# The second feed-forward layer's two products as seven block products each, in two phases with the inner operands in DRAM

## The chip, the cores and the metric

One core of a Trainium2 chip runs the whole program in one launch. The time is device microseconds per execution; the value given is the median of the runs. A profiled execution is a run of its own, and every row below comes from it.

## The reference

Two layers over 1024 latent tokens of width 1024 with 256 context tokens ahead. Each layer is a mixer followed by a squared-ReLU feed-forward part of inner width 4096. The change touches the feed-forward part of the second layer, which sees the 1024 latent tokens alone:

```python
def modulate(x, shift, scale):
    return rms_norm(x) * (1.0 + scale) + shift

def squared_relu_mlp(h, w1, w2):
    return jnp.square(jax.nn.relu(h @ w1)) @ w2
...
# x = x + gate * squared_relu_mlp(modulate(x, shift, scale), w1, w2)
```

All arithmetic is float32. With h as 1024x1024 and w1 as 1024x4096, each of the two products is as large as 4 x 1024^3 multiply-adds.

## The kernel before

Activations are held transposed: eight tiles x (channel blocks of 128 partitions), 1024 tokens along the free dimension. TensorE multiplies in a one-pass 32-bit format, so every float32 operand is split into a high part (a copy by ACT, L94) and a low part (raw minus high, by POOL unless another engine is named, L95), and a product takes three matmuls: high by high, high by low, low by high. `mmk` writes these three for every 512-column chunk (L110).

`wo_phase` ends the mixer: `out_proj` adds the output projection to x one channel block at a time, and `Stats` sums the squares on TensorE. `mlp_layer` then runs the feed-forward part. `norm_mod` multiplies x by rstd on DVE (L226), makes the high part on ACT (L227), the modulated value on DVE (L228) and the low part on POOL (L229), in 16 pieces of 512 columns. `mlp` walks over 32 row blocks f of w1. `first(f, k)` accumulates over the eight channel blocks into two PSUM banks, ACT applies ReLU and the square (L261, L262), DVE makes the low part (L266, L267), and `second(f, c)` multiplies with row f of w2: for each of the eight output blocks three matmuls per chunk into a fresh bank, which DVE adds into x at once (L280). Weights come one row block ahead by `load_w`: one 512 KB transfer on SP's queue, a 1024-wide split on ACT and POOL.

The order of the work on each engine is set by a scheduler from the code, the tile pools and its own estimate of durations; each engine runs its list in order. SP issues all transfers, also in order. PSUM has eight banks, given out in turn.

Of the kernel before, what the change touches and what calls it, by code (L numbers as in the profile page):

```python
# [6 lines left out]
F32 = mybir.dt.float32  # L7
F32R = mybir.dt.float32r
# [962 lines left out]
def mlp_layer(kk, xt, n, mods, w1, w2, segs, stats, side=None, done=None):  # L971

    tc = kk.tc
    with tc.tile_pool(name="MH", reuse_waits="tile", bufs=16) as H:
        kk.slab_w = n
        hs = [tuple(kk.slab(n, F32R, "h", pool=H) for _ in range(2)) for _ in range(KC)]
        with tc.tile_pool(name="MR", reuse_waits="tile", bufs=1) as S, tc.tile_pool(name="MN", reuse_waits="tile", bufs=2) as T:
            kk.S, kk.T = S, T
# [1112 lines left out]
```

## Time and profile before

| | |
|---|---|
| median of 3 runs | 4363.31 us (4356.72 to 4365.94) |
| the profiled execution | 4363.96 us |
| its span | 4362.2 us |
| PE busy | 4064.2 us, 93% |
| DVE, ACT, POOL busy | 59%, 38%, 29% |
| the last feed-forward layer | 3638.0 to the end of the span |

Times in the rows count from the start of the span. In a row of a timeline, the bracket at the end gives the idle time ahead of the instruction and what ended it; `x2` means two instructions merged into one row. PE is the matmul, PEld the weight load that runs beside it, and PEclk the clock that TensorE was granted, 1.00 for 2.4 GHz and 0.50 for 1.2 GHz.

### The profile page before, as it was taken

The numbers are of one execution on the slowest core, as the hardware profiler recorded it, in microseconds if no ns is written. First come the engines' busy times: TensorE is split into PE (matmuls) and PEld (weight loads), VectorE is DVE, ScalarE is ACT, GpSimd is POOL, SyncE is SP. The second block draws the span as 40 slices with busy tenths as digits, with TensorE's granted clock in tenths as the row PEclk, the third lists the DMA queues.
The fourth block names the chain that finished last, engine by engine and source line by source line (L and its number), as shares of the span: only waits on it lengthen the run. The fifth ranks groups of instructions, "written<-read, shape, count | busy, mean of one in ns | idle before, by whom it ended". The sixth has DMA issues, their size and how long they took to land. (4 is left out here: it accounts for less than half of the span.)

```text
span 4362.2 us, 70943 instructions
## 1 busy us (share of the span) xinstructions
PE 4064.2 (93%) x27277; PEld 3262.2 (75%) x27277; DVE 2555.5 (59%) x4810; ACT 1652.6 (38%) x4159; POOL 1280.2 (29%) x1526
## 2 busy tenths in 40 slices
PE   6999998998999999997989985999999998999999
PEld 3899875676777888884757754878777865888887
DVE  4320265517556666668684427678777526666666
ACT  4132365513111111115655533666666632111111
POOL 4112010114111111115533335555545323222221
PEclk9999998999999999998979996999999999999999
DMA  4414344511222111112333454445444431111111
GB/s 171 121 60 138 87 151 140 186 39 33 86 85 63 38 36 39 39 39 70 98 118 111 155 188 114 120 128 136 129 129 130 108 114 44 49 49 49 49 49 63
DMA packets 389183, 409.12 MB, mean 94 GB/s; under 512 B 149884, under 2 KB 305820, under 8 KB 388844
## 3 DMA queue, kind: packets, MB, share of 16 engines
q1 hardware_dynamic: 388844, 404.58, 30.8%
q8 instruction: 215, 3.52, 0.3%
q14 instruction: 124, 1.02, 0.1%
HBM read 304.71 MB, written 95.57 MB: 92 GB/s over the span
## 5 line engine op out<-in xcount | busy, mean ns | idle before, releaser
L280 DVE SCALAR_TENSOR_TENSOR x<-m,mods,x 128x512 f32<-128x512 f32 x1280 | 824.1, 690 | 572.1 <-PE m L110 571.9
L95 POOL TENSOR_TENSOR wl<-raw,wh 128x1024 fp32r<-128x1024 f32 (+1 forms) x236 | 507.6, 2154 | 1919.7 <-ACT wh L94 1872.3
L94 ACT ACTIVATE wh<-raw 128x1024 fp32r<-128x1024 f32 (+1 forms) x236 | 221.7, 940 | 1368.1 <-PE m L110 1068.5
L110 PE MATMUL m<-h,wh 128*128 128x512 f32 (+1 forms) x2560 | 632.2, 375 | 26.9 <-POOL h L229 19.4
L110 PEld LDWEIGHTS m<-h,wh 128*128 128x128 f32 x2560 | 450.2, 189 | 149.5 <-POOL h L229 29.7
L110 PE MATMUL m<-hidh,wh 128*128 128x512 f32 x1280 | 357.8, 372 | 5.7 <-DVE x L280 5.7
L110 PE MATMUL m<-hidl,wh 128*128 128x512 f32 x1280 | 355.5, 371 | 0.8 <-DVE hidl L267 0.7
L110 PE MATMUL m<-hidh,wl 128*128 128x512 f32 x1280 | 352.9, 370 | 0.0
L110 PE MATMUL m<-h,wl 128*128 128x512 f32 x1280 | 352.8, 372 | 0.0
L377 PE MATMUL pt<-wh,h 128*128 128x256 f32 x1600 | 289.3, 283 | 0.0
L110 PEld LDWEIGHTS m<-hidh,wh 128*128 128x128 f32 x1280 | 224.4, 188 | 56.6 <-DVE x L280 13.7
L110 PEld LDWEIGHTS m<-hidl,wh 128*128 128x128 f32 x1280 | 224.8, 188 | 44.6 <-DVE hidl L267 2.2
L110 PEld LDWEIGHTS m<-h,wl 128*128 128x128 f32 x1280 | 225.1, 189 | 42.3
L110 PEld LDWEIGHTS m<-hidh,wl 128*128 128x128 f32 x1280 | 224.4, 188 | 42.9 <-issue 0.5
L377 PEld LDWEIGHTS pt<-wh,h 128*128 128x128 f32 x1600 | 250.0, 192 | 0.0
L1496 DVE TENSOR_TENSOR prd<-P,R 80x31 f32<-80x31 f32 (+15 forms) x496 | 213.5, 430 | 24.8 <-POOL TT L1511 7.8
L377 PE MATMUL pt<-wl,h 128*128 128x256 f32 x800 | 226.4, 283 | 0.0
L1497 DVE TENSOR_TENSOR R<-R,prd 80x31 f32<-80x31 f32 (+15 forms) x496 | 218.6, 441 | 9.6
L1457 PE MATMUL G<-AR,BK 64*128 64x128 f32 x1280 | 173.3, 334 | 22.0 <-POOL AR L1446 10.4
L1018 POOL TENSOR_TENSOR ss<-h 128x512 f32<-128x512 f32 (+1 forms) x128 | 154.5, 1216 | 121.2 <-DVE xt L1021 96.9
L1464 DVE TENSOR_TENSOR G<-G,c_gmask 128x512 f32<-128x512 f32 (+1 forms) x160 | 98.8, 630 | 142.4 <-PE G L1457 142.3
L1457 PEld LDWEIGHTS G<-AR,BK 64*128 64x128 f32 x1280 | 119.8, 209 | 52.6 <-issue 15.9
(403 smaller groups left out, 8203.7 us busy)
## 6 DMA issues: line engine op xcount, KB each, us to landing
raw<-in_w SPq DMA_DIRECT2D x128, 512.0 KB
araw<-in_ada_w SPq DMA_DIRECT2D x80, 512.0 KB
kar<-rw_kar SPq DMA_DIRECT2D x64, 384.0 KB
css<-rw_css SPq DMA_DIRECT2D x80, 256.0 KB
x<-in_xT SPq DMA_DIRECT2D x16, 640.0 KB
raw<-in_w_v SPq DMA_DIRECT2D x20, 512.0 KB
rw_css<-rs SPq DMA_DIRECT2D x16, 640.0 KB
UV<-rw_v SPq DMA_DIRECT2D x80, 128.0 KB
```

The source lines that it names most:

```text
L94: self.nc.scalar.activation(hi, raw, AF.Copy)
L95: (eng or self.nc.gpsimd).tensor_tensor(lo, raw, hi.bitcast(F32), ALU.subtract)
L110: mm(o[:M, :b - a], ww, xx[:, a:b], start=(first and p == 0), stop=(last and p == 2))
L280: V.scalar_tensor_tensor(xt[c][:, u:v], p[:, u - a:v - a], gate[:, c, cond:cond + 1], xt[c][:, u:v], ALU.mult, ALU.add)
L377: mm(ps[:, :n], xx[:, sl], ww[:, k % 4, :], start=(k == 0 and p == 0), stop=(k == KC - 1 and p == 2))
L1018: nc.gpsimd.tensor_tensor(S, h[:, q - 1:q - 1 + w], h[:, q + 1:q + 1 + w], ALU.add)
L1457: nc.tensor.matmul(pg[h][:, 128 * j:128 * j + 128], BK[HH[h], j, :], AR[HH[h], j, :], start=True, stop=True)
L1464: V.tensor_tensor(G[:, :, h, 0:m], ps.rearrange("q (c t) -> q c t", t=128)[:, :, 0:m], mask[:, :, 0:m], ALU.mult)
L1496: V.tensor_tensor(pr, P3[:, s, s + 1:32].unsqueeze(1).to_broadcast([n_, w, n]), R3[:, 0:w, s].unsqueeze(2).to_broadcast([n_, w, n]), ALU.mult)
L1497: V.tensor_tensor(R3[:, 0:w, s + 1:32], R3[:, 0:w, s + 1:32], pr, ALU.add)
```

## The change

The last layer no longer calls `mlp_layer`. `wino_mlp` computes both products with the Strassen-Winograd scheme: each operand is cut into 2x2 blocks, seven block products of sums and differences replace eight, and the results are combined. `h_blocks` makes seven 512x512 operands B out of h, four tiles of 128 partitions each, split into high and low (28 splits, two lows in five on DVE, the others on POOL). `left_first` loads w1 for row blocks f and f+16 and makes the seven weight operands of f on POOL: four combinations and seven 512-wide splits into a ring of seven buffers. `wino_first` runs over 16 f with the seven products in the order SEQ, 12 matmuls each; products that share a combination accumulate in one PSUM bank, with copies by ACT in between (c1, u2, u3). DVE makes the four squared blocks and four differences, and these seven inner operands per f go to DRAM (`hd`). The stores of the last f are held back to the second phase.

`wino_second` runs four steps s over 16 f: two, two, two and one of the seven products, each accumulated over all f in four PSUM banks. In each iteration the operands are read from `hd` and from w2 in halves of 512 columns, combined on DVE and split, w on POOL, the h tiles on POOL and DVE. x is stored to DRAM by `wo_phase` (`xr`) and reloaded at the start of the second phase; at the end of each step DVE adds the finished blocks into it and they go out in halves.

```diff
+SEQ = (0, 1, 5, 4, 6, 3, 2)
+NRING = 7
+WAHEAD = 4
+def triple(kk, o, w, x, first, last):
+    for p, (ww, xx) in enumerate(((w[0], x[0]), (w[0], x[1]), (w[1], x[0]))):
+        kk.nc.tensor.matmul(o, ww, xx, start=(first and p == 0), stop=(last and p == 2), skip_group_check=True)
+def h_blocks(kk, xt, mods, part, rstd, B):
...
+    def norm(c):
+        x = xt[c][:, :NL]
+        V.tensor_tensor(x, x, rstd, ALU.mult)
+        nc.scalar.activation(x, x, AF.Identity, scale=mods[:, 8 * part + 8 + c, 0:1], bias=mods[:, 8 * part + c, 0:1])
+        return x[:, 0:512], x[:, 512:1024]
...
+    for k in range(4):
+        V.tensor_tensor(half(k, 0), half(k, 0), half(4 + k, 0), ALU.subtract)
+        put(3, k, half(k, 0))
...
+def left_first(kk, w1, groups):
...
+        yield wsplit(kk, r1[:, a])
+        s3 = kk.W.tile([128, 512], F32, tag="s3", name="s3", bufs=2)
+        P.tensor_tensor(s3, r1[:, a], r2[:, a], ALU.subtract)
+        yield wsplit(kk, r1[:, b])
+        P.tensor_tensor(r2[:, a], r2[:, a], r2[:, b], ALU.add)
+        P.tensor_tensor(r1[:, a], r2[:, a], r1[:, a], ALU.subtract)
...
+def wino_first(kk, left, groups, B, hd):
...
+        elif p == 6:
+            d["u3"] = copy(d.pop("a"), "u3")
+            d["r22"] = square(f, "r22", d["e"], d["u3"], ALU.add)
+            store(2, f, d["r22"])
...
+            V.tensor_tensor(t1, r12, d["r11"], ALU.subtract)
+            store(4, f, t1)
...
+                w = ws.pop(0)
+                for k in range(4):
+                    triple(kk, d[nm], tuple(t[:, 128 * k:128 * k + 128] for t in w), B[p][k], new and k == 0, k == 3)
+                after(f, p)
...
+def wino_second(kk, w2, hd, late, pool, xr, gate, done):
...
+    prods = ((0, 1), (5, 4), (6, 3), (2,))
...
+        elif s == 1:
+            a, b = t[:, 0:512], t[:, 512:1024]
+            V.tensor_tensor(a, a, b, ALU.add)
+            V.tensor_tensor(b, a, keep[f], ALU.subtract)
+            ws = [wsplit(kk, b), wsplit(kk, a)]
+            V.tensor_tensor(sum4[f], sum4[f], a, ALU.subtract)
...
+        return ws, [wsplit(kk, x, V if j else P) for j, x in enumerate(B)]
...
+    for i in range(LO2):
+        load(i)
+    for d, t in late:
+        nc.sync.dma_start(d, t)
+    ready = [operands(0)]
+    for c in range(KC):
+        nc.sync.dma_start(xt[c], xr[c])
...
@@ -1815,10 +2123,11 @@
-        with tc.tile_pool(name="X", reuse_waits="tile", bufs=1) as X:
-            xt, st = wo_phase(kk, I, d, xd, X, kk.mods[1])
-            with tc.tile_pool(name="W", reuse_waits="tile", bufs=4) as kk.W:
-                mlp_layer(kk, xt, NL, kk.mods[1], I["w1_1"], I["w2_1"], SEG1, st, None, lambda c: nc.sync.dma_start(out[c], xt[c]))
+        xt, st = wo_phase(kk, I, d, xd, X, kk.mods[1], xr)
+        wino_mlp(kk, X, xt, kk.mods[1], I["w1_1"], I["w2_1"], st, xr,
+                 lambda x, c, h: nc.sync.dma_start(out[c][:, 512 * h:512 * h + 512], x))
@@ -1934,8 +2243,9 @@
-        for x in behind(out_proj(kk, I["w_o"], rows(), xt, NL, mods, 2, SEG1, kk.ww), 1):
+        for c, x in enumerate(behind(out_proj(kk, I["w_o"], rows(), xt, NL, mods, 2, SEG1, kk.ww), 1)):
             st.add(x)
+            nc.sync.dma_start(xr[c], x)
```

Three places of the order. The first is POOL at the start of the layer. In its list of before, wl is the low part of a whole weight tile and h a low part of the modulated x:

```order
L1661 TENSOR_TENSOR y_35816<-y_35816,rds 128x512
L1673 TENSOR_TENSOR ro<-ro,gt 128x512 x2
L95 TENSOR_TENSOR wl<-raw,wh 128x1024 x6
L229 TENSOR_TENSOR h<-nt,h 128x512
L95 TENSOR_TENSOR wl<-raw,wh 128x1024 x2
L229 TENSOR_TENSOR h<-nt,h 128x512 x15
L95 TENSOR_TENSOR wl<-raw,wh 128x1024 x60
```

In the list of after, rl is the low part of a weight operand, s and raw are combinations of weights, and b00l is the low part of the first tile of the first h operand:

```order
L1068 TENSOR_TENSOR s_36805<-raw 128x512
L1070 TENSOR_TENSOR raw<-raw 128x512
L1071 TENSOR_TENSOR raw<-raw 128x512
L95 TENSOR_TENSOR rl<-raw,rh 128x512 x2
L1068 TENSOR_TENSOR s_36811<-raw 128x512
L95 TENSOR_TENSOR rl<-raw,rh 128x512
L1070 TENSOR_TENSOR raw<-raw 128x512
L95 TENSOR_TENSOR rl<-raw,rh 128x512
L1071 TENSOR_TENSOR raw<-raw 128x512
L1077 TENSOR_TENSOR raw<-raw 128x512 x2
L95 TENSOR_TENSOR rl<-raw,rh 128x512
L95 TENSOR_TENSOR b00l<-x_35777,b00h 128x512
```

The weight work of the first two row blocks now stands in one piece ahead of the first low part of h.

The second place is PE and ACT within the first two row blocks. ACT of before, where h is the high part of the modulated x and mr and hidh belong to the square:

```order
L227 ACTIVATE h<-nt,mods_70 128x512
L206 ACTIVATE rstd<-rb 128x256
L94 ACTIVATE wh<-raw 128x1024 x2
L227 ACTIVATE h<-nt,mods_70 128x512 x15
L94 ACTIVATE wh<-raw 128x1024
L261 ACTIVATE mr<-m_36627 128x512
```

ACT of after; b33h is the last high part of the h operands in the list, rh the high part of a weight operand:

```order
L94 ACTIVATE b21h<-x_35782 128x512
L94 ACTIVATE b22h<-x_35783 128x512
L94 ACTIVATE b23h<-x_35784 128x512
L94 ACTIVATE b33h<-x_35780 128x512
L94 ACTIVATE rh<-raw 128x512 x2
L1116 ACTIVATE c_36830<-wa 128x512
L1116 ACTIVATE c_36851<-wa 128x512
L94 ACTIVATE rh<-s_36805 128x512
```

PE of before, at the first matmuls of the layer:

```order
L193 MATMUL st<-sq,ones 32x256 x8
L205 MATMUL rb<-r_36511,row_78 128x256 x4
L110 MATMUL m_36627<-h,wh 128x512 x2
L110 MATMUL m_36627<-h,wl 128x512
L110 MATMUL m_36628<-h,wh 128x512
L110 MATMUL m_36635<-h,wh 128x512
L110 MATMUL m_36636<-h,wh 128x512
```

PE of after, behind the first two products (wa and wb); we is the accumulator of the fourth and the last product in SEQ:

```order
L1010 MATMUL wb<-b12h,rl 128x512
L1010 MATMUL wb<-b13h,rh 128x512
L1010 MATMUL wb<-b13l,rh 128x512
L1010 MATMUL wb<-b13h,rl 128x512
L1010 MATMUL we<-b40h,rh 128x512
L1010 MATMUL we<-b40l,rh 128x512
L1010 MATMUL wa<-b50h,rh 128x512
L1010 MATMUL wa<-b50l,rh 128x512
L1010 MATMUL wa<-b50h,rl 128x512
L1010 MATMUL wa<-b51h,rh 128x512
```

The high parts of weights that stood ahead of h on ACT stand behind b33h from the seventh on, and PE's list takes two matmuls of the fourth product, we, ahead of the third, wa.

The third place is SP where the two phases meet. In the list of before SP has one run of weight loads up to the outputs there:

```order
L1933 DMA x_35776<-xd 128x1024
L1913 DMA ct<-rw_cat 128x1024
L90 DMA raw<-in_w_o 128x1024 x2
L90 DMA raw<-in_w_1 128x1024 x64
L1821 DMA out_x<-x_35769 128x1024
L1821 DMA out_x<-x_35770 128x1024
L1821 DMA out_x<-x_35771 128x1024
```

In the list of after, hd_15 are stores of the last row block, k and q halves of w2, x the reload:

```order
L1223 DMA hd_15_36672<-t_39308 128x512
L1223 DMA hd_15_36624<-t_39309 128x512
L1226 DMA x_39358<-xr_35769 128x1024
L1226 DMA x_39359<-xr_35770 128x1024
L1226 DMA x_39360<-xr_35771 128x1024
L1226 DMA x_39361<-xr_35772 128x1024
L1226 DMA x_39362<-xr_35773 128x1024
L1226 DMA x_39363<-xr_35774 128x1024
L1226 DMA x_39364<-xr_35775 128x1024
L1226 DMA x_39365<-xr_35776 128x1024
L1187 DMA k_39322<-in_w_1 128x512
L1187 DMA q_39323<-in_w_1 128x512
```

The last stores and the eight reloads of x stand ahead of the weights of the third iteration of the second phase, which are the k and q in the last two rows.

## Rows read from the trace of the kernel before

**Rows 1.** The page's first part: busy us (share of span) xinstructions.

```profile
PE 4064.2 (93%) x27277; PEld 3262.2 (75%) x27277; DVE 2555.5 (59%) x4810; ACT 1652.6 (38%) x4159; POOL 1280.2 (29%) x1526
```

**Rows 2.** Windows of the last layer's stages: stretch, length, busy by engine, PEclk, DMA.

```profile
core 0: us, PE busy (x) PEld busy (x) DVE busy (x) ACT busy (x) POOL busy (x), PEclk, DMA share, GB/s
3563.50:3625.50 62.00, 62.00 (x261) 43.46 (x260) 5.78 (x9) 7.67 (x18) 2.41 (x2) 1.00 0.03 9
3625.50:3638.00 12.50, 4.62 (x25) 1.47 (x24) 5.46 (x5) 7.60 (x15) 4.65 (x2) 0.79 0.32 88
3638.00:3653.20 15.20, 9.23 (x18) 5.59 (x19) 14.05 (x12) 6.48 (x9) 12.41 (x7) 0.50 0.31 100
3653.20:3687.10 33.90, 27.13 (x110) 19.56 (x108) 28.34 (x30) 13.78 (x20) 23.49 (x14) 1.00 0.10 27
3687.10:4341.50 654.40, 654.40 (x2886) 541.63 (x2887) 424.82 (x605) 121.17 (x177) 139.70 (x58) 1.00 0.15 46
4341.50:4355.30 13.80, 13.80 (x62) 11.12 (x60) 13.74 (x22) 0.82 (x2) 0.00 (x0) 1.00 0.36 148
4355.30:4362.20 6.90, 0.05 (x1) 0.00 (x0) 3.24 (x5) 0.00 (x0) 0.00 (x0) 0.82 0.77 313
```

**Rows 3.** The chain of waits, two pieces: start us, us, what.

```profile
3687.08 654.45 PE m L110 x2885
...
4356.57 1.98 DVE x L280 x3
```

**Rows 4.** Groups by line, 3600 to 4362: busy us, mean ns, idle before.

```profile
L280 DVE SCALAR_TENSOR_TENSOR x<-m,mods,x 128x512 f32<-128x512 f32 x512 | 356.7, 744 | 229.6 <-PE m L110 229.6
L110 PE MATMUL m<-h,wh 128*128 128x512 f32 x1024 | 279.7, 393 | 14.7 <-POOL h L229 9.8 <-ACT h L227 4.8
...
L110 PE MATMUL m<-h,wl 128*128 128x512 f32 x512 | 159.6, 392 | 0.0
...
L266 DVE TENSOR_TENSOR mr<-mr 128x512 f32<-128x512 f32 x64 | 60.5, 983 | 5.6 <-ACT hidh L262 5.6
...
L261 ACT ACTIVATE mr<-m 128x512 f32<-128x512 f32 x64 | 34.3, 588 | 18.9 <-PE m L110 18.9
```

**Rows 5.** Timeline of POOL, 3630 to 3650: start us, us, operation.

```profile
3631.92 4.65 POOL L95 TENSOR_TENSOR wl<-raw,wh 128x1024 fp32r<-128x1024 f32 x2 [57.06 <-ACT wh L94]
...
3640.22 5.57 POOL L95 TENSOR_TENSOR wl<-raw,wh 128x1024 fp32r<-128x1024 f32 x2
```

**Rows 6.** Timeline of DVE, 3598 to 3700.

```profile
3638.46 7.89 DVE L226 TENSOR_TENSOR nt<-x,rstd 128x512 f32<-128x512 f32 x4
...
3656.15 0.68 DVE L226 TENSOR_TENSOR nt<-x,rstd 128x512 f32<-128x512 f32 x1
```

**Rows 7.** Groups by line and shape, the whole span.

```profile
L94 ACT ACTIVATE wh<-raw 128x512 fp32r<-128x512 f32 x64 | 39.9, 625 | 60.5 <-PE po L1065 34.5 <-PE pv L1266 13.3 <-DMA raw<-in_rkv 7.9
...
L1653 POOL TENSOR_TENSOR y<-y,rds 128x512 f32<-128x512 f32 x16 | 18.8, 1178 | 4.2 <-DVE rds L1652 3.3 <-POOL vt L1649 0.3
...
L534 DVE TENSOR_TENSOR raw<-raw,rope 128x1024 f32<-128x1024 f32 x8 | 9.7, 1218 | 0.0
```

**Rows 8.** Timeline of ACT, 3633 to 3645.

```profile
3633.99 0.94 ACT L206 ACTIVATE rstd<-rb 128x256 f32<-128x256 f32 x3 [1.21 <-PE rb L205]
...
3640.45 1.06 ACT L94 ACTIVATE wh<-raw 128x1024 fp32r<-128x1024 f32 x1 [1.27 <-DMA raw<-in_w]
```

**Rows 9.** Timeline of SP's DMA issues, 3630 to 3640 and 4340 to 4362.

```profile
3634.29 2.63 SPq L90 DMA_DIRECT2D raw<-in_w  x2
...
4349.35 9.55 SPq L1821 DMA_DIRECT2D out_x<-x  x8
```

**Rows 10.** Window with the reload of x by the output projection.

```profile
3520.00:3530.00 10.00, 10.00 (x37) 7.92 (x37) 9.00 (x21) 4.17 (x6) 3.44 (x3) 0.82 1.06 387
```

**Rows 11.** Timeline of PE, end of the output projection.

```profile
3619.79 0.63 PE L110 MATMUL wo<-cth,wh 128*128 128x512 f32 x2
...
3624.92 0.63 PE L110 MATMUL wo<-cth,wl 128*128 128x512 f32 x2
```

More of the change, by code (lines that the diff above doesn't have):

```diff
@@ L982, in mlp_layer, with wsplit, wraw @@
             mlp(kk, xt, n, hs, w1, w2, mods[:, 40:48, :], segs, side, done)
+SEQ = (0, 1, 5, 4, 6, 3, 2)
+NRING = 7
+WAHEAD = 4
+HTAGS = ("c1", "u2", "u3", "r11", "r21", "r22")
+def wsplit(kk, src, eng=None):
+    hi, lo = (kk.W.tile([128, 512], F32R, tag=t, name=t, bufs=NRING) for t in ("rh", "rl"))
+    kk.split(src, hi, lo, eng)
+    return hi, lo
+def wraw(kk, src):
+    t = kk.W.tile([128, 1024], F32, tag="raw", name="raw", bufs=4)
+    kk.nc.sync.dma_start(t, src)
+    return t
+def triple(kk, o, w, x, first, last):
+    for p, (ww, xx) in enumerate(((w[0], x[0]), (w[0], x[1]), (w[1], x[0]))):
+        kk.nc.tensor.matmul(o, ww, xx, start=(first and p == 0), stop=(last and p == 2), skip_group_check=True)
@@ new lines, in h_blocks, with put @@
+def h_blocks(kk, xt, mods, part, rstd, B):
+    nc = kk.nc
+    V, P = nc.vector, nc.gpsimd
+    n = [0]
+    def put(p, k, src):
+        n[0] += 1
+        hi, lo = B[p][k]
+        kk.split(src, hi, lo, V if n[0] % 5 in (0, 2) else P)
+    def norm(c):
[4 more added lines that the diff above has]
+    for k in range(4):
+        put(0, k, norm(k)[0])
+    for k in range(4):
+        put(1, k, norm(4 + k)[0])
+    half = lambda c, i: xt[c][:, 512 * i:512 * i + 512]
+    for k in range(4):
+        t = kk.tmp([128, 512], "n1", bufs=2)
+        V.tensor_tensor(t, half(k, 1), half(k, 0), ALU.subtract)
+        V.tensor_tensor(half(k, 0), half(4 + k, 1), t, ALU.subtract)
+        put(5, k, half(k, 0))
+        put(4, k, t)
+    for k in range(4):
+        P.tensor_tensor(half(k, 1), half(4 + k, 1), half(k, 1), ALU.subtract)
+        put(6, k, half(k, 1))
+    for k in range(4):
+        V.tensor_tensor(half(k, 0), half(k, 0), half(4 + k, 0), ALU.subtract)
+        put(3, k, half(k, 0))
+    for k in range(4):
+        put(2, k, half(4 + k, 1))
@@ new lines, in left_first, with load, one @@
+def left_first(kk, w1, groups):
+    P = kk.nc.gpsimd
+    raws = {}
+    fs = [f for g in groups for f in g]
+    def load(f):
+        if f < 16:
+            raws[f] = [wraw(kk, w1[g].rearrange("q k m -> q (k m)")) for g in (f, f + 16)]
+    load(0)
+    def one(f):
+        if f not in raws:
+            load(f)
+        r1, r2 = raws.pop(f)
+        a, b = slice(0, 512), slice(512, 1024)
+        yield wsplit(kk, r1[:, a])
[4 more added lines that the diff above has]
+        P.tensor_tensor(r1[:, a], r2[:, a], r1[:, a], ALU.subtract)
+        yield wsplit(kk, r1[:, a])
+        yield wsplit(kk, r2[:, a])
+        load(f + 1)
+        yield wsplit(kk, s3)
+        yield wsplit(kk, r2[:, b])
+        P.tensor_tensor(r1[:, b], r1[:, b], r1[:, a], ALU.subtract)
+        yield wsplit(kk, r1[:, b])
+    for g in groups:
+        gens = [one(f) for f in g]
+        for _ in SEQ:
+            for x in gens:
+                yield next(x)
@@ new lines, in wino_mlp @@
+def wino_mlp(kk, X, xt, mods, w1, w2, stats, xr, done):
+    tc = kk.tc
+    kk.W = tc.alloc_tile_pool(name="WW", reuse_waits="tile", bufs=1, side="right")
+    H = tc.alloc_tile_pool(name="WH", reuse_waits="tile", bufs=1, side="right")
+    B = [None] * 7
+    for p in SEQ:
+        B[p] = [tuple(H.tile([128, 512], F32R, name="b%d%d%s" % (p, k, x)) for x in "hl") for k in range(4)]
+    groups = [(0, 1)] + [(f,) for f in range(2, 16)]
+    left = left_first(kk, w1, groups)
+    hd = [[kk.dram.tile([128, 512], F32, name="hd%d_%d" % (p, f), tag="hd%d_%d" % (p, f)) for f in range(16)] for p in range(7)]
+    kk.slab_w = NL
+    with tc.tile_pool(name="WN", reuse_waits="tile", bufs=1) as kk.S:
+        kk.T = kk.S
+        h_blocks(kk, xt, mods, 3, stats.rstd(), B)
+    X.release()
+    with tc.tile_pool(name="WT", reuse_waits="tile", bufs=2) as kk.T:
+        late = wino_first(kk, left, groups, B, hd)
+        H.release()
+        with tc.tile_pool(name="WK", reuse_waits="tile", bufs=1, side="right") as pool:
+            wino_second(kk, w2, hd, late, pool, xr, mods[:, 40:48, :], done)
+    kk.W.release()
@@ L1817, in build_full @@
         d = layer1_mixer(kk, I, xt, X, kk.mods[1], st1)
-        with tc.tile_pool(name="X", reuse_waits="tile", bufs=1) as X:
-            xt, st = wo_phase(kk, I, d, xd, X, kk.mods[1])
-            with tc.tile_pool(name="W", reuse_waits="tile", bufs=4) as kk.W:
-                mlp_layer(kk, xt, NL, kk.mods[1], I["w1_1"], I["w2_1"], SEG1, st, None, lambda c: nc.sync.dma_start(out[c], xt[c]))
+        X = tc.alloc_tile_pool(name="X", reuse_waits="tile", bufs=1)
+        xr = [dr.tile([128, NL], F32, name="xr%d" % c, tag="xr%d" % c) for c in range(KC)]
+        xt, st = wo_phase(kk, I, d, xd, X, kk.mods[1], xr)
+        wino_mlp(kk, X, xt, kk.mods[1], I["w1_1"], I["w2_1"], st, xr,
+                 lambda x, c, h: nc.sync.dma_start(out[c][:, 512 * h:512 * h + 512], x))
 RC = ["mu", "w0", "a0", "k_k", "k_a", "lnx_w", "lnx_b", "rks", "sel", "gmask"]
```

144 lines of the change are left out of this document (143 added, 1 removed).

## The prediction, made before the kernel ran

> **What bounds the kernel now.** I read the page's busy shares first: TensorE is busy 93% of the span and no other engine above 59% [rows 1]. The windows by stage then show where that holds [rows 2]. In the last feed-forward layer there is a ragged start from 3638.0, a stretch of 654.4 us with PE busy all of it at granted clock 1.00, and an end of 6.9 us in which PE does nothing. The chain of waits says the same: one piece, 654.45 us, 2885 matmuls [rows 3], so 226.8 ns each. The layer has 1024 + 4 x 512 = 3072 matmuls [rows 4]. Of these 2885 are in that piece, 62 behind it [rows 2], so 125 came before 3687.1; they needed 28.4 us of work and took 49.1. So 20.7 us are lost at the start, and the rest is matmul count times 226.8 ns. The end is VectorE's: its last additions run after the last matmul, the last of the eight output transfers is issued by 4358.9, 3.3 us before the end [rows 9].
>
> **What the change removes.** Each product is now 7 x 16 x 12 = 1344 matmuls, so 2688 instead of 3072. All have the same 128x512 shape, each with its own weight load. The 384 that go are worth 384 x 0.2268 = 87.1 us, the most that can be won on PE. VectorE also loses the 512 additions of 744 ns out of PSUM [rows 4]. The instruction order on every engine is unchanged up to the last eight steps of the output projection, so everything before 3626 stays.
>
> **Start of the layer, the largest loss.** Three steps.
> (a) POOL now does 14 weight operations (six lows, eight combinations) ahead of the first low part of h, b00l. The nearest price is the first pair of 1024-wide subtractions, 4.65 us for two with VectorE out of the way [rows 5]; a 512-wide POOL operation took 1178 ns [rows 7]. When VectorE ran products with two SBUF operands beside them, two such POOL subtractions took 5.57 us [rows 5], and four 512-wide VectorE products took 7.89 us, where one alone takes 0.68 [rows 6]. So they take turns: a 512-wide VectorE operation adds (5.57 - 4.65)/2 = 0.46 us to POOL, and a pair of 512-wide ones, one on each, costs 1.18 + 0.46 = 1.64 us. A 1024-wide VectorE product (1218 ns [rows 7], 0.53 more than the 0.68) makes the pair 2.15 us.
> ACT's rstd copies began at 3633.99 [rows 8]; four 512-wide splits of 625 ns [rows 7] now stand between them, so the first norm starts at about 3638. By then POOL, from about 3631.5, has done 5 or 6 of its 14. The other eight or nine take turns with eight 1024-wide norms and one split: 8 x 2.15 + 1.64 = 18.8, so b00l starts near 3657. Until then PE can do one matmul.
> (b) After that POOL has 21 and VectorE 22 operations before all seven h operands exist, 1.64 us a pair. PE does the first two products as their parts come, 46 matmuls, and then meets a matmul of the fourth product whose weight ACT splits only behind b33h. b33h needs VectorE's twentieth operation: 3657 + 20 x 1.64 = 3690, plus two ACT splits of 0.6, so about 3691.5.
> (c) From there 168 - 46 = 122 matmuls of the first pair of row blocks remain, 27.7 us. PE has then stood for some 20 us. Before, the granted clock was 0.50 (the 1.2 GHz level) from 3638.0 to 3653.2 [rows 2] after a similar gap, with PE starved most of the time. I allow 2 to 3 us for slow matmuls and get 3722 for the end of the first pair.
> PE thus loses 3722 - 3638 - 168 x 0.2268 = 46 us here against 20.7 before. Bounds: 3700, if weights and h are ready some 20 us earlier because the turns cost less; 3735, if each wait adds a little.
>
> **The rest of phase one.** 14 row blocks of 84 matmuls, 19.05 us each. Per block POOL has 11 operations (7 lows, 4 combinations), VectorE 8 with two SBUF operands and 4 out of PSUM. Taking turns: 8 x 1.64 + 3 x 1.18 = 16.7 us of POOL. ACT's ten take 6.2. Transfers are 1 MB of weights and 1.8 MB of intermediates per block, 150 GB/s, where 387 was reached [rows 10]. All hidden under PE, by 2.4 us in the tightest case. I add 3 us for copies that PE waits for: the accumulator of the sixth product must be copied out of PSUM (0.59) and added (0.74) within one product, 2.72 [rows 4].
> The Trainium skill (SBUF — State Buffer, Who interferes with whom) has a rule that speaks against this change: a VectorE instruction with two SBUF inputs and a GpSimd instruction that reads SBUF exclude each other for the whole instruction. By that rule the trace agrees: the turns above are what it describes, and the change puts eight such operations per block beside eleven of POOL.
>
> **The seam between the phases.** SP is one queue. The third iteration's weights (k, q) now stand behind the last stores of phase one, and behind the reload of x, 8 x 512 KB. Call the last matmul of phase one T. The first weights' transfers are issued when block 15's third square is done, T - 1.2, and land about 3 us later: the second of two 512 KB loads, issued by 3636.92 [rows 9], was ready for ACT at 3640.45 [rows 8], 3.5 us, and these have half the size. ACT and POOL then split three tiles before the second matmul can run: T + 1.8 + 0.6 + 3 x 1.18 = T + 6. Two iterations of 24 matmuls give T + 17. The last store waits for VectorE's r12, four differences and one weight combination, about T + 6.5. 4.45 MB at 387 GB/s [rows 10] take 11.5, k and q land at T + 20.5, their lows and that of the h tile follow: T + 25. That is 25 - 11 = 14 us lost, plus 2 for the slower clock after two gaps: 16 us. Bounds 5 (if the reload starts early) and 30.
>
> **Phase two and the end.** Per iteration 24 matmuls, 5.44 us. POOL has 3 splits, VectorE 2 operations with two SBUF operands in steps one and three (4.46 us by turns), 4 in step two: 3 x 1.64 + 0.6 = 5.5, above 5.44. With seven buffers in the ring this is nearly serial: 4 us over step two. Step four has 2 POOL splits in 2.72 us. Changing banks between steps: 2 us. At the end the additions keep pace with PE, and 256 KB instead of 512 go out last: 4.4 us behind the last matmul instead of 6.9.
>
> **Sum.** 3722 + 2520 x 0.2268 (571.5) + 3 + 16 + 4 + 2 + 4.4 = 4322.9, against a span of 4362.2: 39 us less. The profiled execution took 4363.96, 0.65 above the median of the runs, 4363.31. Median after: 4363.3 - 39 = 4324.
> One price has two rows: in the output projection twelve pairs run from 3619.79 to 3624.92, 233 ns a matmul at clock 1.00 [rows 2, 11], not 226.8. I take 226.8, since the matmuls of this layer had it; the other would add 2520 x 0.0064 = 16 us.
> The Trainium skill (TensorE: Matmul & The Clock Gate, Wait — 56ns, not 53.3ns?) gives 215.7 ns for a warm 512-column matmul; by that the 2520 would take 543.6 us. The trace differs: 226.8, and the measurement decides.
>
> **Rivals.**
> 1. Slower: the turns of VectorE and POOL become the bound. The point is 19.05 us a block, a pair of 1.94 us instead of 1.64. If all 12 VectorE operations hold POOL up for their 0.68, a block takes 11 x 1.18 + 12 x 0.68 = 21.1, 2.1 x 14 = 29 us more; an iteration of phase two 3 x 1.18 + 4 x 0.68 = 6.3, 0.8 x 48 = 39 more. Less the 4 counted: 4324 + 64 = 4388. For it: VectorE's L266 takes 983 ns on average beside POOL [rows 4]. Against it: L280, with one SBUF operand, keeps 744.
> 2. The start or the seam costs less: the first pair done at 3700, seam 14: 4300.
> 3. Matmuls at 233 ns: 4340.
> 4. The queue at the seam costs twice, 32 us: 4340.
> That the change would not do what it says is excluded by the order: PE has 384 instructions fewer.
>
> **How the numbers follow.** A difference below 0.2% (8.7 us) counts as none. Forecast, within 4308 to 4338: 0.48. Rivals: 2 0.13, 3 0.11, 4 0.10, 1 0.18. Of rival 1, 0.11 ends above 4372 and 0.07 in between, since a little over the point costs 30 us. Of 3 and 4 together with other small losses 0.02 end within 0.2%. Faster 0.80, same 0.09, slower 0.11. The range leaves out rival 1 and the best of rival 2: 4296 to 4356.
>
> **What would show it.** In the trace of after: the first long run of PE at about 3692 and its second block pair at 3722; blocks 19.05 us apart; one PE gap of some 6 and one of some 8 us at the seam, released by POOL's lows behind k and q; step two slightly over 87 us. The forecast is wrong if blocks are over 20 us apart with PE waiting for POOL, or if PE runs densely before 3680.

## The result and the profile after

The changed kernel took 4329.08 us (median of 8 runs, 4320.61 to 4349.31), the kernel before beside it 4360.02 (8 runs, 4347.85 to 4366.05). The medians are 31 us apart. The ratio is 0.9934, with a 95% interval of 0.9914 to 0.9955: 0.66% faster, clear of noise but small. The forecast was 4324, within 4296 to 4356, and as a difference 39 us.

The profiled execution had a span of 4322.0 us against 4362.2, 40 us less, but 9 of these lie ahead of the layer. ScalarE's first rstd copy, which opens the layer, began at 3624.92, and before at 3633.99 [rows 8]; ahead of it both kernels issue the same work but for eight stores, and in the executions below that copy lies anywhere from 3623.1 to 3638.6, so the 9 us are within what differs from one execution to the next. So from here on times count from that copy, and are called "behind rstd". From it to the end the layer took 728.2 us before and 697.1 after: 31.1 less, what the medians say. By the same count the forecast was 688.9.

The windows by stage of the changed kernel (columns as in [rows 2]; the last row is a short stretch of phase two):

```profile
core 0: us, PE busy (x) PEld busy (x) DVE busy (x) ACT busy (x) POOL busy (x), PEclk, DMA share, GB/s
3644.60:3662.70 18.10, 15.08 (x48) 10.03 (x48) 17.60 (x12) 13.74 (x19) 15.50 (x10) 0.83 0.01 1
3662.70:3681.90 19.20, 0.15 (x1) 0.00 (x0) 18.05 (x14) 8.64 (x16) 16.68 (x12) 0.64 0.00 0
...
3752.00:3983.90 231.90, 231.90 (x1024) 191.80 (x1022) 158.82 (x151) 67.77 (x115) 182.72 (x125) 1.00 0.47 160
3983.90:4013.00 29.10, 17.32 (x59) 13.08 (x59) 20.66 (x18) 8.35 (x15) 16.97 (x12) 0.82 1.01 370
...
4104.70:4108.20 3.50, 3.50 (x9) 2.73 (x10) 2.44 (x4) 0.00 (x0) 0.00 (x0) 0.52 0.65 195
```

They answer [rows 2]. In the first row PE does 48 matmuls, in the second it stands for 19.2 us. The third is a stretch of 231.9 us in which PE is busy all the time. Around 3983.9 lies the seam, with the transfer engines at 100%. In the last row, behind a gap of 4 us, the granted clock is 0.52.

The page's first part, and the longest piece of the chain, answer [rows 1] and [rows 3]:

```profile
PE 3980.1 (92%) x26893; PEld 3190.9 (74%) x26893; DVE 2516.8 (58%) x4533; ACT 1756.3 (41%) x4379; POOL 1654.3 (38%) x1819
```

```profile
4193.89 89.56 PE w L1010 x388
```

PE has 84.1 us less busy time, near the 87.1 expected (busy time overlaps and holds slow matmuls), and it is still what runs longest, but the chain now has one piece of 89.56 us where before it had 654.45. 388 matmuls in 89.56 us are 230.8 ns each with the slow ones in it; twelve of phase one's blocks took 19.04 us for 84, which is 226.7.

Where the time of the layer goes, from the starts of the matmuls (us; the pure work is 3072 or 2688 matmuls of 0.2268):

| | before | forecast | after |
|---|---|---|---|
| pure work | 696.7 | 609.6 | 609.6 |
| lost up to the end of the first pair (before: ahead of the end) | 24.6 | 49.9 | 50.3 |
| lost in the other 14 blocks | | 3 | 3.8 |
| lost at the seam | | 16 | 16.2 |
| lost in phase two behind it | | 6 | 13.3 |
| behind the last matmul | 6.9 | 4.4 | 3.9 |
| layer | 728.2 | 688.9 | 697.1 |

So of the 87.1 us of matmuls that are gone, 56 are given back. The experiments ask what takes them.

### The profile page after: what moved, and what is told of

Same layout as the page of the kernel before. It is cut to its first block, busy times and chain, and to the rows that moved or that the text cites. A ratio compares the mean times of both kernels' runs of the same rounds, so it can differ in the third digit from the quotient of the medians.

```text
span 4322.0 us, 71491 instructions
## 1 busy us (share of the span) xinstructions
PE 3980.1 (92%) x26893; PEld 3190.9 (74%) x26893; DVE 2516.8 (58%) x4533; ACT 1756.3 (41%) x4379; POOL 1654.3 (38%) x1819
## 5 line engine op out<-in xcount | busy, mean ns | idle before, releaser
L280 DVE SCALAR_TENSOR_TENSOR x<-m,mods,x 128x512 f32<-128x512 f32 (+1 forms) x768 | 467.6, 656 | 341.0 <-PE m L110 340.7
L110 PE MATMUL m<-h,wh 128*128 128x512 f32 (+1 forms) x1536 | 352.5, 362 | 12.2 <-POOL h L229 9.7
L110 PEld LDWEIGHTS m<-h,wh 128*128 128x128 f32 x1536 | 256.3, 189 | 88.8 <-issue 26.8
L95 POOL TENSOR_TENSOR rl<-raw,rh 128x512 fp32r<-128x512 f32 x160 | 241.0, 1515 | 119.4 <-ACT rh L94 119.2
L110 PE MATMUL m<-hidh,wh 128*128 128x512 f32 (+1 forms) x768 | 198.3, 360 | 1.9 <-DVE x L280 1.9
L110 PE MATMUL m<-hidl,wh 128*128 128x512 f32 (+1 forms) x768 | 195.6, 358 | 0.3 <-DVE hidl L267 0.3
L110 PE MATMUL m<-hidh,wl 128*128 128x512 f32 (+1 forms) x768 | 193.8, 357 | 0.0
L110 PE MATMUL m<-h,wl 128*128 128x512 f32 (+1 forms) x768 | 193.0, 359 | 0.0
L1010 PE MATMUL w<-rl,rh 128*128 128x512 f32 x448 | 178.5, 399 | 11.8 <-DVE rl L95 7.7
L1010 PE MATMUL w<-rh 128*128 128x512 f32 x448 | 176.9, 395 | 7.8 <-ACT rh L94 7.8
```

The lines of the kernel that those rows point to most:

```text
L95: (eng or self.nc.gpsimd).tensor_tensor(lo, raw, hi.bitcast(F32), ALU.subtract)
L110: mm(o[:M, :b - a], ww, xx[:, a:b], start=(first and p == 0), stop=(last and p == 2))
L280: V.scalar_tensor_tensor(xt[c][:, u:v], p[:, u - a:v - a], gate[:, c, cond:cond + 1], xt[c][:, u:v], ALU.mult, ALU.add)
L1010: kk.nc.tensor.matmul(o, ww, xx, start=(first and p == 0), stop=(last and p == 2), skip_group_check=True)
```

## The experiments

Only the layer's time is compared where a kernel has a single execution, since the part ahead of it differs by several microseconds from one execution to the next. The layer's own time moves a little too, so such a run is read at the place that its edit touches.

### The reload of x later

```diff
-    for c in range(KC):
-        nc.sync.dma_start(xt[c], xr[c])
...
         load(i + LO2)
+        if 3 <= i < 3 + KC:
+            nc.sync.dma_start(xt[i - 3], xr[i - 3])
```

> The reload of x (eight 512 KB transfers) is issued one per iteration behind the loads of iterations 3 to 10 of phase two, instead of ahead of the third iteration's weights. Theory (SP's order): in the changed kernel the third iteration's weights k and q were issued at 3995.03, behind 4.9 us of reload; now they are issued some 5 us earlier, the two PE gaps of 2.44 and 2.48 us in iteration 2 and the slow clock behind them go, iteration 2 takes 5.4 to 6 us instead of 9.35, and the phase starts 4 us shorter. The first two gaps (6.13 and 2.79 us) stay, since they hang on the first weights' landing and POOL's first lows. Rival (POOL and the port): POOL needs 1.7 us for each of three lows per iteration whenever VectorE works beside it, so iteration 2 still takes over 8 us.

SP's queue in the changed kernel, first the reload, then the third iteration's first weight:

```profile
3990.06 4.92 SPq L1226 DMA_DIRECT2D x<-xr  x8
3995.03 0.43 SPq L1187 DMA_DIRECT2D k<-in_w  x1
```

PE at the seam and behind it in the changed kernel (the bracket is the idle time and what ended it):

```profile
3983.57 0.39 PE L1010 MATMUL we<-b23h,rl 128*128 128x512 f32 x1
3989.70 0.79 PE L1010 MATMUL w<-rh 128*128 128x512 f32 x1 [5.75 <-ACT rh L94]
3992.50 0.79 PE L1010 MATMUL w<-rl,rh 128*128 128x512 f32 x1 [2.00 <-POOL rl L95]
...
4006.99 0.51 PE L1010 MATMUL w<-rh 128*128 128x512 f32 x1 [2.06 <-ACT rh L94]
4009.47 0.79 PE L1010 MATMUL w<-rl,rh 128*128 128x512 f32 x1 [1.98 <-POOL rl L95]
...
4104.70 0.67 PE L1010 MATMUL w<-rl,rh 128*128 128x512 f32 x1 [3.56 <-DVE rl L95]
```

The first two gaps are the ones ended at 3989.70 and 3992.50, the next two at 4006.99 and 4009.47. Gaps in the text, here and below, are counted from the start of one matmul to the start of the next, so they are a little longer than the bracket. In the run with the later reload, k of the third iteration was issued right behind the last stores:

```profile
3994.66 0.44 SPq L1187 DMA_DIRECT2D k<-in_w  x1
```

That is 365.5 us behind rstd, where it was 370.1. Iterations 0, 1 and 2 took 10.63, 5.44 and 5.44 us, where they took 9.63, 7.66 and 9.35, and the first gaps stayed (6.30 and 3.24). From the last matmul of phase one to the end of iteration 2 it is 27.8 us instead of 32.8. The layer took 693.1, 4.0 less. The theory holds: SP's order cost 5 of the seam's 16 us. The other 11 lie at the first weights; what would take them away was not tested by itself, only in the last run below, together with other edits.

### The additions behind the low splits, in two forms

```diff
-                done(add(c, 0, v[c]), c, 0)
+                todo.append(lambda c=c: done(add(c, 0, v[c]), c, 0))
...
             ready.append(operands(i + 1))
+        if f < 15 and todo:
+            todo.pop(0)()
```

Both forms have these lines. The first has these too:

```diff
-            V.tensor_tensor(sum4[f], sum4[f], a, ALU.subtract)
+            more = lambda: kk.tc.keep_in_program_order(V.tensor_tensor(sum4[f], sum4[f], a, ALU.subtract))
...
+        if s == 1:
+            more()
```

> VectorE's additions into x at the ends of steps one and two are issued one per iteration of the next step, each behind that iteration's low split, and the update of the fourth weight (q minus raw) behind the low split too; no operation is left out. Theory (VectorE's queue): the gaps of 3.95 us in iteration 18 and 4.49 us in iteration 33 of phase two, both ended by a VectorE low split, are the wait behind these additions; they go together with the slow clock behind them, both iterations take 5.5 to 6 us instead of 10.9 and 11.3, and phase two is 9 to 11 us shorter. Rival (the port in step two): step two has four VectorE operations and three of POOL an iteration, 3 x 1.70 + 0.61 = 5.71 us by turns, above PE's 5.44, and four additions more; then the wait only spreads over step two, which still takes 93 to 97 us (94.1 before), and only the gap of iteration 33 goes, 5 to 6 us in all.

> As the run with additions behind the lows, but the update of the fourth weight stays where it was; only the additions into x at the ends of steps one and two are issued one per iteration of the next step, behind its low split. In that run VectorE waited 4 us an iteration for raw weights, because the moved update held their buffers. Theory (VectorE's queue): both gaps ended by a VectorE low split go, iterations 18 and 33 take 5.5 to 6 us instead of 10.9 and 11.3, phase two is 8 to 11 us shorter than in the changed kernel. Rival (the port in step two, 5.71 us an iteration by turns): step two still takes 92 to 95 us (94.1 before), its wait only spread over more iterations, and 4 to 6 us are won at iteration 33 alone.

VectorE's timeline in the changed kernel around the two gaps shows what stands ahead of the low split that PE waits for:

```profile
4086.98 2.72 DVE L1243 SCALAR_TENSOR_TENSOR x<-v,mods,x 128x512 f32<-128x512 f32 x2
...
4102.30 1.74 DVE L1211 TENSOR_TENSOR q<-q,raw 128x512 f32<-128x512 f32 x1
4103.97 0.68 DVE L95 TENSOR_TENSOR rl<-u,rh 128x512 fp32r<-128x512 f32 x1
...
4184.00 3.48 DVE L1243 SCALAR_TENSOR_TENSOR x<-u,mods,x 128x512 f32<-128x512 f32 x2
...
4193.16 0.68 DVE L95 TENSOR_TENSOR rl<-u,rh 128x512 fp32r<-128x512 f32 x1
```

At the first gap these are the reads of the finished banks, four additions into x and six combinations, most at the 1.7 us that a turn with POOL takes; at the second, eight additions, two of them in the row of 3.48 us.

In the first form the layer took 710.5 us, 13 more. Both theories missed that. The update of the fourth weight reads the raw buffer, and when it is moved back the buffer comes free later; VectorE then waits for the load, and PE for VectorE, in most iterations of step two. VectorE's timeline in that run:

```profile
4158.38 0.69 DVE L1208 TENSOR_TENSOR raw<-raw 128x512 f32<-128x512 f32 x1 [4.25 <-DMA raw<-in_w]
```

In the second form the layer took 689.7, 7.4 less. Iteration 33 fell from 11.27 to 5.44, and step three from 92.87 to 87.04, which is 16 x 5.44: with the additions out of the way nothing is lost there. Step two fell only from 94.09 to 92.28, as the rival said: its 10.88 at iteration 18 became 6.95 and 7.38 at iterations 18 and 20, and seven iterations still took 5.61 to 5.73. That is the 3 x 1.70 + 0.61 = 5.71 of three turns and one operation alone. So of the 7 us that step two lost, nearly 2 were the additions' place in the queue.

The queue alone is not the cause, though. In the run with all on VectorE (below) the additions stand where they stood in the changed kernel, and step two lost 2.2 us, step three 0.9. There the same eight additions take 0.70 us each, two of them in this row of VectorE's timeline:

```profile
4158.87 1.41 DVE L1243 SCALAR_TENSOR_TENSOR x<-u,mods,x 128x512 f32<-128x512 f32 x2
```

With both, in the last run, step two lost 0.3 us and step three nothing. So the gap in iteration 33 needs the additions ahead of the low split and POOL beside them, which makes each about 1.74 us long; to take away either is almost enough. In step two 5 of the 7 us go with POOL.

### TensorE in the sequence of the products

```diff
-        kk.nc.tensor.matmul(o, ww, xx, start=(first and p == 0), stop=(last and p == 2), skip_group_check=True)
+        m = kk.nc.tensor.matmul(o, ww, xx, start=(first and p == 0), stop=(last and p == 2), skip_group_check=True)
+        if pin:
+            kk.tc.keep_in_program_order(m)
```

> TensorE's matmuls of the first pair of row blocks keep the order of the products (1st, 2nd, third, fourth ...); in the changed kernel two matmuls of the fourth product stood ahead of the third product's 24 and waited for a weight that ScalarE split only behind the last part of h. Theory (one misplaced pair of matmuls): PE now does the third product as its parts of h come, so the gap of 19.45 us breaks up, and the first pair ends 4 to 6 us earlier than at 88.4 us behind the first rstd copy. Rival (the parts of h bound it): the third product's last parts of h come so late, and the slower clock after the starved stretch costs so much, that the end of the pair moves by less than 1.5 us.

The first pair's last matmul started 88.2 us behind rstd, as without the edit, and the layer took 699.9, 2.8 more, most of it in later blocks, which the edit does not touch. The theory falls; the rival has the number right and not the reason, and the timelines of PE and of ScalarE in this run show why:

```profile
3686.94 0.80 PE L1010 MATMUL wa<-b50h,rh 128*128 128x512 f32 x1 [18.52 <-ACT c L1118]
```

```profile
3684.73 0.63 ACT L94 ACTIVATE b33h<-x 128x512 fp32r<-128x512 f32 x1 [0.70 <-DVE x L1046]
...
3686.31 1.06 ACT L1118 ACTIVATE c<-wa 128x512 f32<-128x512 f32 x2
```

The third product adds into the bank of the first (`d["a"]` is one bank for products 0, 5 and 6), so its first matmul waits until `copy` has read that bank. ScalarE's copy is queued behind b33h, the last of the 28 high parts of h. The same holds in the changed kernel, where the copy stands right behind the rows that the prediction named (ScalarE's timeline):

```profile
3641.14 0.63 ACT L94 ACTIVATE rh<-raw 128x512 fp32r<-128x512 f32 x1 [12.55 <-POOL raw L1071]
...
3680.71 0.63 ACT L94 ACTIVATE b33h<-x 128x512 fp32r<-128x512 f32 x1 [0.70 <-DVE x L1044]
3681.24 1.14 ACT L94 ACTIVATE rh<-raw 128x512 fp32r<-128x512 f32 x2
3682.28 1.06 ACT L1116 ACTIVATE c<-wa 128x512 f32<-128x512 f32 x2
```

The first of these rows is another wait in ScalarE's queue: 12.55 us for a combination by POOL, with ScalarE's part of the norms (scale and shift) and all high parts of h behind it.

### The copies ahead

```diff
+    yield
+    pin[0] = True
...
+                if g is groups[0] and p == 0:
+                    nc.scalar.activation(cx[f], d["a"], AF.Copy)
+                    d["c1"] = cx[f]
...
+            if g is groups[0] and p == 1:
+                yield more, ws
```

The first `yield` stands behind the first eight tiles of h (two operands); from there on `pin` keeps each high part at its place in the sequence.

> In the head ScalarE copies the first product's two accumulators out of PSUM directly behind b13h, and the splits of the other five operands of h, with four weights of the first pair between them, keep their sequence behind these copies; engines of all operations unchanged (the differences n are kept in rstd's buffer, the differences t have one buffer each). Theory (ScalarE's queue): the third product adds into the bank that the copy must read first, and the copy stood behind all 20 splits of h, so PE waited 19 us whatever stood first in its own sequence; now PE does the third and fourth products while h is still made, the 19 us gap breaks into short ones, and the first pair ends 74 to 78 us behind the first rstd copy instead of 88.2. Rival (turns at the port): the parts of h come no sooner, PE waits for them instead, and the pair still ends behind 84.

The gap of 19 us broke up, and PE began its 156th matmul at 75.3 us instead of 82.9. Then it waited 5.4 us more, and the pair's last matmul started at 84.8. PE's timeline in this run, and ScalarE's:

```profile
3689.97 0.79 PE L1010 MATMUL wa<-b52l,rh 128*128 128x512 f32 x1 [3.84 <-POOL b52l L1026]
...
3719.34 0.79 PE L1010 MATMUL we<-b20h,rh 128*128 128x512 f32 x1 [5.04 <-DVE r L1114]
```

```profile
3716.93 1.15 ACT L94 ACTIVATE rh<-raw 128x512 fp32r<-128x512 f32 x2 [9.86 <-POOL raw L1077]
3717.99 0.58 ACT L1122 ACTIVATE u<-wa 128x512 f32<-128x512 f32 x1
```

First PE waits for the third product's parts of h (3.8 us for b52h, then 4.5 for its low by POOL), as the rival said, and then for a square behind a copy that is queued on ScalarE, this time behind a split of the next block's weight that waits 9.86 us for POOL. The next block then ran in 19.04 us instead of 22.47, so 6.7 us were left at the end of phase one, and the layer took 690.5, 6.6 less. The theory had the wait right and its worth wrong: POOL has the work of the head in turns with VectorE, and that comes no sooner.

### All on VectorE

```diff
-    kk.split(src, hi, lo, eng)
+    kk.split(src, hi, lo, kk.nc.vector)
...
-        kk.split(src, hi, lo, V if n[0] % 5 in (0, 2) else P)
+        kk.split(src, hi, lo, V)
...
-    P = kk.nc.gpsimd
+    P = kk.nc.vector
```

> Every operation that POOL did in this layer (low splits and combinations of weights and h, lows of phase two) is issued to VectorE instead; POOL does nothing there. Theory (turns at the port cost more than they give): a VectorE operation 512 wide takes 0.61 us when POOL is silent, a pair of one each 1.70. In the head some 58 operations of 0.61 and eight norms of 1.13 make 44 us instead of 61, so the last low of h comes at about 45 us behind the first rstd copy instead of 60, and the first pair ends 12 to 18 us earlier. Blocks of phase one stay at 19.05 us (VectorE 19 x 0.61 + 4 x 0.72 = 14.5 us), the seam is 3 to 5 us shorter, step two runs at 5.44 us an iteration. In all 18 to 27 us faster than the changed kernel, near 4304 us. Rival (POOL is a second worker that VectorE needs): VectorE's queue then holds weights' lows behind squares that wait for PE, blocks take 20 us or more, and the kernel is slower than the changed one, above 4335 us.

4305.72 us (4 runs), a ratio of 0.9878 (0.9837 to 0.9920) to the kernel before; the layer took 671.0, 26 less than in the changed kernel. The first pair's last matmul started 68.2 us behind rstd instead of 88.2; 11.8 of these 20 us are won up to the first matmul, which started at 7.9 instead of 19.7. The blocks stayed at 19.04, and step two fell to 89.28, not to the 87 expected. The seam lost 15.2 us for 16.2, where 3 to 5 less were expected. VectorE's timeline shows operations back to back:

```profile
3634.51 4.63 DVE L1026 TENSOR_TENSOR x<-x,rstd 128x1024 f32<-128x1024 f32 x4
...
3669.48 0.69 DVE L95 TENSOR_TENSOR b23l<-x,b23h 128x512 fp32r<-128x512 f32 x1
```

In the changed kernel five norms took 10.14 us and POOL's operations 2.24 each beside them, as VectorE's and POOL's timelines there show:

```profile
3628.62 10.14 DVE L1026 TENSOR_TENSOR x<-x,rstd 128x1024 f32<-128x1024 f32 x5 [5.01 <-ACT rstd L206]
3645.10 1.47 DVE L95 TENSOR_TENSOR b01l<-x,b01h 128x512 fp32r<-128x512 f32 x1 [6.34 <-ACT b01h L94]
...
3680.60 1.77 DVE L95 TENSOR_TENSOR b20l<-x,b20h 128x512 fp32r<-128x512 f32 x1
3682.29 1.77 DVE L95 TENSOR_TENSOR b22l<-x,b22h 128x512 fp32r<-128x512 f32 x1
```

```profile
3637.65 2.24 POOL L95 TENSOR_TENSOR rl<-raw,rh 128x512 fp32r<-128x512 f32 x1
...
3641.07 2.49 POOL L1077 TENSOR_TENSOR raw<-raw 128x512 f32<-128x512 f32 x2
...
3644.74 1.29 POOL L95 TENSOR_TENSOR b00l<-x,b00h 128x512 fp32r<-128x512 f32 x1
...
3681.77 1.74 POOL L95 TENSOR_TENSOR b23l<-x,b23h 128x512 fp32r<-128x512 f32 x1
3683.47 1.75 POOL L95 TENSOR_TENSOR b33l<-x,b33h 128x512 fp32r<-128x512 f32 x1
```

With all on VectorE four norms take 4.63. Later in the head of the changed kernel a low starts every 1.7 us on either engine, each with a record of 1.74 to 1.77; the two at 3641.07 ran while VectorE stood idle. The last low of h is begun 38.7 us behind rstd (b23l) instead of 58.6 (b33l). Two things did not shrink. PE still stood 15.8 us ahead of the third product, for the same copy, and a new wait of 6.48 us came up in step four, whose lows now stand on VectorE behind the twelve additions that end step three. PE's timeline at both places:

```profile
3667.76 0.80 PE L1010 MATMUL wa<-b50h,rh 128*128 128x512 f32 x1 [15.44 <-ACT c L1116]
...
4255.09 0.80 PE L1010 MATMUL w<-rl,rh 128*128 128x512 f32 x1 [6.09 <-DVE rl L95]
```

One rival was not tried: POOL kept, but the weight work of the second row block moved behind the first parts of h. What it would win of the 11.8 us ahead of the first matmul is open.

### Four more subtractions

```diff
-            V.tensor_tensor(t1, r12, d["r11"], ALU.subtract)
+            for _ in range(2):
+                V.tensor_tensor(t1, r12, d["r11"], ALU.subtract)
... (t2, t3 and t4 alike)
```

> Each of the four VectorE differences of a row block of phase one is issued twice (same inputs, same output): VectorE has 12 operations with two SBUF operands a block instead of 8, POOL its 11. Theory (turns at the port): 11 pairs of 1.70 and one of 0.61 make 19.3 us, and what VectorE's four reads of PSUM (0.69 each) don't overlap comes on top; blocks of phase one go from 19.04 to between 19.5 and 22 us with PE waiting for POOL's lows, 7 to 40 us in all. Rival (the engines overlap, VectorE has room): VectorE is busy 68% of a block, 2.7 us more fit, and blocks stay at 19.04.

With the first pair as blocks one and two, those from the fourth to the fourteenth took 19.04 to 20.40 us, 19.36 on average; two others had single waits of 10.5 and 4.3 us, and phase one ended 21.1 us later. What PE waited for at the longest of these was not a low of POOL, as expected, but a square by VectorE, which stands behind the differences of the block before:

```profile
3745.65 0.79 PE L1010 MATMUL we<-b20h,rh 128*128 128x512 f32 x1 [10.11 <-DVE r L1108]
```

Groups by line in these blocks (busy us, mean ns, idle before):

```profile
L95 POOL TENSOR_TENSOR rl<-raw,rh 128x512 fp32r<-128x512 f32 x59 | 100.5, 1721 | 0.9 <-ACT rh L94 0.9
...
L1139 DVE TENSOR_TENSOR t<-r,r 128x512 f32<-128x512 f32 x20 | 34.3, 1717 | 0.3
...
L1142 DVE TENSOR_TENSOR t<-r,t 128x512 f32<-128x512 f32 x20 | 21.0, 1052 | 0.3
...
L1108 DVE TENSOR_TENSOR r<-we,u 128x512 f32<-128x512 f32 x20 | 13.8, 688 | 6.3 <-PE we L1010 5.3 <-ACT u L1116 0.9
```

By line, VectorE's operations with two SBUF operands take 1.05 to 1.72 us on average beside POOL, one that reads PSUM keeps 0.69. The engines do take turns, and with 8 + 4 operations beside POOL's 11 the blocks are no longer free of it. That the average of 19.36 lies so near the 19.3 from the count of turns proves little: five of the eleven blocks stayed at 19.04, and most of the 21.1 us came with the two single waits. Eight operations leave a reserve: 8 x 1.70 + 3 x 1.25 = 17.4 us of POOL by the measured prices, 1.7 below the block's 19.04, where the prediction had 2.4.

### All of it together

The kernel has all on VectorE, the copies ahead, the later reload, the additions of all steps behind the lows, and:

```diff
+        if g is groups[-1]:
+            for i, t in enumerate(cx):
+                nc.sync.dma_start(t, w2[16 * (i % 2) + i // 2][:, 0, 0:512])
...
-    keep, sum4 = zip(*[(half("k%d" % f), half("q%d" % f)) for f in range(16)])
+    keep = [cx[2 * f] if f < 2 else half("k%d" % f) for f in range(16)]
+    sum4 = [cx[1] if f == 0 else half("q%d" % f) for f in range(16)]
```

> All on VectorE, together with the copies ahead in the head, the reload of x one per iteration from the fourth on, the additions into x of steps one to three one per iteration of the next step, and the first weights of phase two (k0, q0, k1) loaded before the last row block into buffers of their own. Theory (what is lost is turns at the port plus single waits in the queues of ScalarE, SP and VectorE): against all on VectorE alone the first pair ends 12 to 15 us earlier (53 to 57 us behind the first rstd copy instead of 68.2), the two gaps at the seam (5.7 and 5.0 us with slow clock behind) shrink to 2 us or less, 8 to 11 us, and the gap of 6.5 us at step four goes: 4271 to 4284 us, 1.8 to 2.0% below the kernel before. Rival (VectorE is dense in the head and bounds it alone): no more than 3 us from the copies, and 4285 to 4295 us.

4269.88 us (5 runs, 4261.92 to 4276.98), a ratio of 0.9791 (0.9769 to 0.9813) to the kernel before: 2.1% faster, and faster than the changed kernel, whose interval lies above this one. The median lies 1 us below the range expected. Its windows at the seam and behind it (the seam, phase two):

```profile
3954.00:3962.00 8.00, 6.59 (x29) 4.84 (x27) 5.88 (x10) 3.23 (x6) 0.00 (x0) 1.00 0.83 300
3962.00:4260.90 298.90, 298.90 (x1317) 247.06 (x1317) 209.28 (x331) 126.91 (x221) 0.00 (x0) 1.00 0.57 187
```

The first pair's last matmul starts 59.1 us behind rstd, somewhat later than the 53 to 57 expected. Phase two's first matmul starts 0.22 us behind phase one's last, at clock 1.00, and 2.1 us in all are lost behind that. The layer took 637.3 us, 90.9 less than before: nothing of the 87.1 is given back. Besides its matmuls it loses 27.7 us, where the kernel before lost 31.5.

For the head the runs make a square (start of the first pair's last matmul, us behind rstd; the last kernel's further edits lie behind the head):

| | copies behind h | copies ahead |
|---|---|---|
| POOL and VectorE | 88.2 | 84.8 |
| VectorE alone | 68.2 | 59.1 |

POOL's part is worth 20 to 26 us, the copy 3 to 9, and each is worth more when the other is gone.

## Why the prediction was right, and where it was off

The parts of the forecast hold where the loss lies: at the start, at the seam and little between. That two of the sums hit to half a microsecond is luck, since errors inside them cancel; the difference to the kernel before came out 8 us smaller than forecast, 31 for 39.

**Matmuls removed: right.** Blocks of 19.04 us are 84 x 226.7 ns; rival 3, 233 ns, is out. The Trainium skill (TensorE: Matmul & The Clock Gate, Wait — 56ns, not 53.3ns?) has 215.7 ns; these rows disagree with it after the change as before.

**Start, (a) to (c): size right by offsets, one link wrong.** b00l was expected 23 us behind rstd and was begun at 19.8; a pair of 512-wide operations took 1.70 us, not 1.64, one of 1024 and one of 512 2.20, not 2.15; b33h was expected at 56.0 and came at 55.8, and PE resumed at 57.0 for 57.5. So (a) was 3.2 us too long and the stretch from b00l to b33h 3.0 too short, 33.0 for 36.0, and they cancel. In (a) eight norms were to take turns with POOL; it was five, because VectorE then stood 6.3 us for b01h, which was queued on ScalarE behind the split that waited 12.55 us for POOL. The pair's end was expected at 88.0 and came at 88.4, its last matmul starting at 88.15. Step (b), though, gave as the reason "a matmul of the fourth product whose weight ACT splits only behind b33h". PE did wait for that weight, but it is only what stood first in PE's sequence: with it put back PE waits as long, for the copy of the first product's bank, which the prediction did not place at all. Both sit directly behind b33h in ScalarE's queue, so the time came out right with the wrong name on it.

**The rest of phase one: right.** 14 blocks took 270.5 us for 269.7. POOL is hidden in the later ones. Of the 3.8 us lost 3.4 are the first of these blocks, where PE waits for a copy out of PSUM that is queued on ScalarE behind a weight split; a wait of 2.63 for a square by VectorE fell into the first pair.

**The seam: sum right by offsets.** 16.2 for 16. The wait up to the second matmul was 8.5 us for 6, that of the third iteration 4.5 for 8 (2.44 and 2.48, less a matmul's 0.23 each), and the slower clock took 3.3 for 2. The reload's place in SP's queue was worth 5. The rest lies at the first weights: with POOL left out alone the seam still lost 15.2, and with these weights loaded early as well, and the reload later, it is gone. Their early load was not tested by itself.

**Phase two: the term that was mis-sized.** "Changing banks between steps: 2 us" was 7.6: 5.8 at step three and 1.8 at step two, where additions into x stand ahead of a low split on VectorE. The prediction looked at the banks and not at who else queues where they are read, and at what price: beside POOL the eight additions of step three cost 5.8, with POOL silent 0.9. "4 us over step two" from the turns was 5.2 (its own working, 0.08 us over 16 iterations, gives 1.3; the 4 is more than what it is worked out from), and half a microsecond was lost in step four: 13.3 for 6. This is most of the 8.2 us by which the layer's 697.1 exceeds the forecast's 688.9.

**Rival 1: not reached, but near.** The blocks stood 4 VectorE operations short of it, and step two was past it in seven iterations. A turn was priced nearly right, 1.64 for 1.70; what the prediction did not ask is what the turns cost in all. It took them as given in its 46 us at the start, and never set them against the same work on VectorE alone, which ends the first pair 20 us earlier.

## What to carry to other kernels

Before work is shared between VectorE and POOL, compare the pair by turns with both operations on VectorE: here 1.70 us against 1.21, so the second engine made the head 20 us longer. Where a stage starts, follow each engine's queue and not only the operands: a copy out of PSUM, an addition nobody waits for or a reload can each stand ahead of the one instruction that TensorE needs. Moving such an instruction back also moves the release of the buffers it reads.

## What was not expected of the hardware

Two 512-wide operations took 1.21 us on VectorE with POOL silent, and 1.70 us as one on each engine (the lows at 3680.60 to 3683.47 above); POOL alone needs 1.24 to 1.26 for one (the two at 3641.07). These three had not been put side by side. On VectorE with POOL silent four start 0.60 us apart, in the run with all on VectorE:

```profile
3676.10 1.29 DVE L95 TENSOR_TENSOR rl<-s,rh 128x512 fp32r<-128x512 f32 x2
3677.30 1.29 DVE L95 TENSOR_TENSOR rl<-raw,rh 128x512 fp32r<-128x512 f32 x2
```
The Trainium skill (GPSIMD Engine Reference, Engine selection) says to give elementwise work to VectorE, because GpSimd is about twice as slow with two inputs; the runs agree, 1.24 us against 0.61, and add that sharing the work was slower here than leaving POOL out. The Trainium skill (SBUF — State Buffer, Who interferes with whom) states an exclusive lock between a VectorE instruction with two SBUF inputs and a GpSimd instruction that reads SBUF; the records of 1.74 to 1.77 us on both engines, against 1.25 and 0.69 alone, agree with it.

The groups by line in the changed kernel's undisturbed blocks show the same without any edit:

```profile
L1109 DVE SCALAR_TENSOR_TENSOR r<-r 128x512 f32<-128x512 f32 x50 | 57.2, 1144 | 1.7
...
L1140 DVE TENSOR_TENSOR t<-r,t 128x512 f32<-128x512 f32 x12 | 20.2, 1687 | 0.0
...
L1108 DVE TENSOR_TENSOR r<-we,u 128x512 f32<-128x512 f32 x24 | 16.6, 692 | 67.0 <-ACT u L1116 59.3 <-PE we L1010 7.7
```

VectorE's L1140, beside POOL in eleven of its twelve records, takes 1687 ns on average; L1109 takes 1144, with records from 0.69 to 1.84 us; and L1108, which reads PSUM and mostly runs beside POOL too, keeps 692.

Each long wait also costs behind its end: after the gap of 3.95 us that ended at 4104.70 the granted clock was at its lower level (0.52 in the 3.5 us behind it, near the 0.50 of 1.2 GHz), and the clock's part of the seam was 3.3 us. In the run with all edits the seam's window shows 1.00.
